# The activation sums of the seven-product scheme, all on DVE and all ahead of the first pair

## The chip, the cores and the metric

One core of a Trainium2 chip runs the whole kernel. The metric is device time in microseconds, median of several executions. The engines are named as in the profile: PE (TensorE, with PEld for its weight loads), DVE (VectorE), ACT (ScalarE), POOL (GpSimd) and SP (SyncE, whose queue issues loads).

## What is computed

The reference is one layer of a hybrid encoder on 1024 sample rows and 256 prompt rows with shared weights. The part that matters here is the MLP's first product:

```python
h2 = rms_norm(x, norm_mlp_g) * (1 + scale2) + shift2      # 1280 x 1024
x = x + gate2 * (jnp.square(jax.nn.relu(h2 @ w_mlp_up)) @ w_mlp_down)   # w_mlp_up 1024 x 4096
```

## The kernel before, in words

All large products are made from pairs: a float32 matrix is kept as a high and a low half (`h`, `l`), and each product takes three matmuls (h·h, h·l, l·h). h2, transposed, lies in `Mh[c]`, `Ml[c]` as 8 blocks k of 128 rows; chunk c = 0 and 1 are 512 sample rows each, c = 2 the 256 prompt rows.

The up product runs over 16 pairs of 128-column weight blocks. Pairs 0 and 1 are done plainly. From pair 2 on, chunks 0 and 1 together are a 2 x 2 block product done with seven block products in place of eight (`up_pair`, L1446): the activations' four blocks, B11, B21 (chunk 0, k 0 to 3 and 4 to 7), B12 and B22 (chunk 1), are combined once into T1 = B12 - B11, T2 = B22 - T1, T3 = B22 - B12 and T4 = B21 - T2, each again as high and low halves, and serve all 14 pairs. T3 is written over the first half of `Mh[1]`, `Ml[1]`. The weights' sums (`p_sum`, `p_split`) are made anew for each pair.

A set's block k (128 x 512) is made by: one sum of halves for each source block (`b_raw`, L1376, gives the float32 value back), a subtraction on DVE, a copy to the high half on ACT (`t_split`, L1389), and the low half on DVE (`t_lo`, L1390), which is issued later in the order so that DVE need not wait for ACT's copy. `t_first(k)` makes T1 and T2, `t_third(k)` T3, `t_fourth(k)` T4. Before the change, `b_raw` gives the sums of B11, B22 and B21 to POOL and that of B12 to DVE. `t_fourth` makes T2's float32 value anew from its halves, on POOL (L1413). The sums lie in a ring of five tiles of 128 x 512, `r_tile`, which also holds the up product's outputs on their way to HBM.

The order of work on each engine is written out by hand: each engine takes its instructions in program order. `t_first(0)` to `(3)` and `t_third(0)`, `(1)` stand between the evictions (`up_out`: relu, square and a DMA, all on ACT) of pairs 0 and 1 and the weight splits of pair 2 (`p_ab`: copy on ACT at L156, low half `wl` on POOL at L160). The rest stands inside pair 2, in the function `after(step)` which `up_pair` calls between its products: `t_third(2)`, `t_third(3)` after step 0, `t_fourth(0)`, `(1)` after step 1, `t_fourth(2)`, `(3)` after step 2.

In `up_pair` three small steps hold PE up if they are late. `p1` (L1457), a copy on ACT of the first product in its PSUM bank, must be made before PE adds the second product to that bank; `u2` (L1467) and `q` (L1473), DVE sums of another bank with p1, must be made before PE adds to that bank. `p1`, `u2` and `q` have one tile each in the pool `ev`. PE's work while the T sets are made is the plain products of pairs 0 and 1, then pair 2's.

Of the kernel before, what the change touches and what calls it, by code (L numbers as in the profile page):

```python
# [7 lines left out]
F32 = mybir.dt.float32  # L8
F32R = mybir.dt.float32r
AF = mybir.ActivationFunctionType  # L10
ALU = mybir.AluOpType
# [59 lines left out]
def encoder_kernel(tc, x_prompt, x_sample, c_prompt, c_sample, ada_w, ada_b, norm_mix_g, w_in,  # L71
# [3 lines left out]
    nc = tc.nc  # L75
# [10 lines left out]
    def pool(name, bufs=1, side=None, space=None):  # L86
        kw = {}
        if side:
            kw["side"] = side
        if space:  # L90
            kw["space"] = space
        if space != bass.MemoryType.DRAM:
            kw["reuse_waits"] = "tile"
        cm = tc.tile_pool(name=name, bufs=bufs, **kw)
        return cm, cm.__enter__()
# [610 lines left out]
    for part in (1, 0):  # L706
        for t in range(NT):
# [22 lines left out]
            if part == 0 and t in (2, 5):  # L730
                k = t // 3
# [256 lines left out]
    ev = {}  # L988
# [101 lines left out]
    for g in range(len(TT) + 8):  # L1090
# [5 lines left out]
        if 2 <= g < len(TT) + 2:  # L1096
            n, k = TT[g - 2]
# [13 lines left out]
    Mh = [(mcp if c == 2 else mxp).tile([128, KD, n], F32R, name=f"Mh{c}") for c, (_, n) in enumerate(CH)]  # L1111
    Ml = [(mcp if c == 2 else mxp).tile([128, KD, n], F32R, name=f"Ml{c}") for c, (_, n) in enumerate(CH)]
# [152 lines left out]
    def plain(out, ws, fi, c):  # L1265
        for k in range(KD):
            wh, wl = ws[k // 4]
            cols = slice(fi * 128, fi * 128 + 128)
            passes(out, wh[:, k % 4, cols], wl[:, k % 4, cols], Mh[c][:, k, :], Ml[c][:, k, :], k == 0, k == KD - 1)

    def up_bank():
        return bank("b", "up_ps", 8)
# [19 lines left out]
    ev_cm, ev = pool("ev", side="left")  # L1292
# [20 lines left out]
    def r_tile(name="r"):  # L1313
        return ev.tile([128, 512], F32, tag="r", name=name, bufs=5)
# [5 lines left out]
    def up_out(f, c, src, r=None):  # L1320
        r = r_tile() if r is None else r
        relu_sq(r, src)
        nc.scalar.dma_start(up_d[f][:, c * 512:c * 512 + 512], r)

    def up_out_c2(i, src):
        r = r_tile()
        relu_sq(r, src)
        for fi in range(2):
            nc.scalar.dma_start(up_d[2 * i + fi][:, 1024:T], r[:, fi * 256:fi * 256 + 256])
# [10 lines left out]
    def p_sum(i, second):  # L1340
        ra, rb = prep[i]["raw"]
        a11, a21, a12, a22 = ra[:, :, 0:128], ra[:, :, 128:256], rb[:, :, 0:128], rb[:, :, 128:256]
        s = wu.tile([128, 2, 4, 128], F32, tag="sr", name="sr", bufs=2)
        if second:
            nc.vector.tensor_tensor(s[:, 0], a11, a21, op=ALU.subtract)
            nc.vector.tensor_tensor(s[:, 1], a12, prep[i]["s12"][:, 1], op=ALU.subtract)
            prep[i]["s34"] = s
        else:
            nc.vector.tensor_tensor(s[:, 0], a21, a22, op=ALU.add)
            nc.vector.tensor_tensor(s[:, 1], s[:, 0], a11, op=ALU.subtract)  # L1350
            prep[i]["s12"] = s

    def p_split(i, second):
        prep[i]["w"]["S34" if second else "S12"] = split_w(prep[i]["s34" if second else "s12"], [128, 2, 4, 128])
# [18 lines left out]
    TT_ = {n: [Tp.tile([128, 4, 512], F32R, name=f"T{n}{x}") for x in "hl"] for n in (1, 2, 4)}  # L1373
    TT_[3] = [Mh[1][:, 0:4, :], Ml[1][:, 0:4, :]]

    def b_raw(c, k, e):  # L1376
        t = r_tile("br")
        e.tensor_tensor(t, Mh[c][:, k, :].bitcast(F32), Ml[c][:, k, :].bitcast(F32), op=ALU.add)  # L1378
        return t

    late_lo = []
# [1 line left out]
    def t_lo():  # L1383
        while late_lo:
            late_lo.pop(0)()

    def t_split(n, k, t):
        h, l = TT_[n][0][:, k, :], TT_[n][1][:, k, :]
        nc.scalar.activation(h, t, AF.Copy)  # L1389
        late_lo.append(lambda: nc.vector.tensor_tensor(l, t, h.bitcast(F32), op=ALU.subtract))  # L1390

    def t_first(k):
        b11 = b_raw(0, k, nc.gpsimd)
        b12 = b_raw(1, k, nc.vector)
        t_lo()
        b22 = b_raw(1, k + 4, nc.gpsimd)
        nc.vector.tensor_tensor(b11, b12, b11, op=ALU.subtract)
        t_split(1, k, b11)
        nc.vector.tensor_tensor(b22, b22, b11, op=ALU.subtract)
        t_lo()  # L1400
        t_split(2, k, b22)

    def t_third(k):
        b22 = b_raw(1, k + 4, nc.gpsimd)
        b12 = b_raw(1, k, nc.vector)
        t_lo()
        nc.vector.tensor_tensor(b22, b22, b12, op=ALU.subtract)
        t_split(3, k, b22)

    def t_fourth(k):  # L1410
        b21 = b_raw(0, k + 4, nc.gpsimd)
        t2 = r_tile("br")
        nc.gpsimd.tensor_tensor(t2, TT_[2][0][:, k, :].bitcast(F32), TT_[2][1][:, k, :].bitcast(F32), op=ALU.add)  # L1413
        nc.vector.tensor_tensor(b21, b21, t2, op=ALU.subtract)
        t_lo()
        t_split(4, k, b21)

    t_first(0)
    up_out(1, 0, po[1, 0])
    t_first(1)  # L1420
# [11 lines left out]
    up_out_c2(1, pm1)  # L1432
    p_sum(2, True)
    t_third(1)
    t_lo()
    up_out(2, 0, po[2, 0])
    up_out(3, 0, po[3, 0])

    def prod(out, w, at_, xh, xl, first, last, more=False):

        for k in range(4):
            a, b = k == 0 and first, k == 3 and last
            for s, (l_, r_) in enumerate(((at_(w[0], k), xh), (at_(w[0], k), xl), (at_(w[1], k), xh))):
                nc.tensor.matmul(out, lhsT=l_, rhs=r_[:, k, :], start=(a and s == 0), stop=(b and s == 2),  # L1444
                                 skip_group_check=more)

    def up_pair(i, after):
        w = prep[i]["w"]
        f0 = lambda t, k: t[:, k, 0:128]
        f1 = lambda t, k: t[:, k, 128:256]  # L1450
        s0 = lambda t, k: t[:, 0, k, :]
        s1_ = lambda t, k: t[:, 1, k, :]
        B = {(r, c): [M[c][:, 4 * r:4 * r + 4, :] for M in (Mh, Ml)] for r in range(2) for c in range(2)}
        X = up_bank()
        prod(X, w["A"], f0, *B[0, 0], True, False, True)
        p1 = ev.tile([128, 512], F32, tag="p1", name="p1", bufs=1)
        nc.scalar.activation(p1, X, AF.Copy)  # L1457
        after(0)
        pm = up_bank()
        plain(pm[:, 0:256], (w["A"], w["B"]), 0, 2)  # L1460
        prod(X, w["B"], f0, *B[1, 0], False, True, True)
        up_out(2 * i, 0, X)
        after(1)
        Y = up_bank()
        prod(Y, w["S12"], s1_, *TT_[2], True, False, True)
        u2 = ev.tile([128, 512], F32, tag="u2", name="u2", bufs=1)
        nc.vector.tensor_tensor(u2, Y, p1, op=ALU.add)  # L1467
        V = up_bank()
        prod(V, w["S12"], s0, *TT_[1], True, False, True)
        after(2)  # L1470
        prod(Y, w["S34"], s0, *TT_[3], False, False, True)
        q = ev.tile([128, 512], F32, tag="q", name="q", bufs=1)
        nc.vector.tensor_tensor(q, Y, p1, op=ALU.add)  # L1473
        c22 = r_tile()
        nc.vector.tensor_tensor(c22, V, q, op=ALU.add)
        plain(pm[:, 256:512], (w["A"], w["B"]), 1, 2)
        up_out(2 * i + 1, 1, c22, c22)
        up_out_c2(i, pm)
        after(3)
        prod(Y, w["B"], f1, *TT_[4], False, True, True)  # L1480
        c21 = r_tile()
        nc.vector.tensor_tensor(c21, Y, p1, op=ALU.add)
        up_out(2 * i + 1, 0, c21, c21)
        after(4)
        prod(V, w["S34"], s1_, Mh[1][:, 4:8, :], Ml[1][:, 4:8, :], False, True, True)
        c12 = r_tile()
        nc.vector.tensor_tensor(c12, V, u2, op=ALU.add)
        up_out(2 * i, 1, c12, c12)
        after(5)
# [27 lines left out]
    for i in range(2, NP):  # L1517
        last = i == NP - 1

        def after(step, i=i, last=last):  # L1520
            if i == 2 and step == 0:
                t_third(2)
                t_third(3)
            elif i == 2 and step < 3:
                t_fourth(2 * step - 2)
                t_fourth(2 * step - 1)
                t_lo()
            if step == 0:
                p_split(i, True)
                if last:  # L1530
                    wd_load(0)
                    wd_load(1)
                    g_load(0)
                else:
                    p_load(i + 1)
            elif step == 1:
                wd_split(0) if last else p_ab(i + 1, 0)
            elif step == 2:
                g_load(1) if last else p_sum(i + 1, False)
            elif step == 3:  # L1540
                g_split(0) if last else p_sum(i + 1, True)
            elif step == 4:
                wd_split(1) if last else p_ab(i + 1, 1)
            elif not last:
                p_split(i + 1, False)
        up_pair(i, after)
# [188 lines left out]
```

## Time and profile before

| | before |
|---|---|
| median of 3 runs | 1913.94 us (1913.16 to 1914.57) |
| the profiled execution | 1914.83 us |
| its span | 1912.9 us |
| PE, DVE, ACT, POOL busy | 97%, 56%, 36%, 37% |
| mean granted clock of PE | 0.985 |

Durations below come from the one profiled execution; its own time is 0.9 us above the median. In a row of the timeline, the first number is the start in us, the second the duration, and the bracket at the end is the idle time before it and what ended it. The granted clock is a share of full speed: 1.00 is 2.4 GHz, 0.50 is 1.2 GHz.

### The profile page before, as it was taken

How to read it: one execution, taken by the hardware profiler on the slowest of the kernel's cores; microseconds unless marked ns; L12 is line 12 of the kernel's file. 1: busy time of each engine (PE TensorE's matmuls, PEld its weight loads, DVE VectorE, ACT ScalarE, POOL GpSimd, SP SyncE). 2: the span in 40 equal slices, each digit the busy share in tenths (PEclk: the TensorE clock that was granted, in tenths of full speed). 3: DMA queues.
4: the chain of work that ended last, by engine and by line, in shares of the span. 5: the costliest groups of instructions: out<-in, count | busy, mean ns of one | idle time of the engine just before them, and what ended most of it. 6: DMA issues, size and time to landing. Idle time of an engine off the chain costs nothing.

```text
span 1912.9 us, 24543 instructions
## 1 busy us (share of the span) xinstructions
PE 1852.5 (97%) x9468; PEld 1545.5 (81%) x9468; DVE 1067.1 (56%) x1374; ACT 682.5 (36%) x1132; POOL 698.5 (37%) x517
## 2 busy tenths in 40 slices
PE   5999999999999999999999979999999999999998
PEld 2888777888997888877788868888888888888886
DVE  2799995533446777776445543333324555555557
ACT  3401111221346778773223434444444211111111
POOL 3321121421322333447312543333335543344343
PEclk7999999999999999999999989999999999999999
DMA  8313452237140212127632223222335432233224
GB/s 310 111 45 110 166 185 97 70 111 241 47 129 32 57 37 54 35 75 234 196 112 82 68 72 100 94 88 90 98 99 172 158 97 65 87 99 100 70 97 153
DMA packets 120934, 207.55 MB, mean 108 GB/s; under 512 B 10946, under 2 KB 78355, under 8 KB 119794
## 3 DMA queue, kind: packets, MB, share of 16 engines
q1 hardware_dynamic: 103106, 167.32, 27.5%
q10 hardware_dynamic: 17712, 38.67, 5.1%
q8 instruction: 74, 1.21, 0.3%
q14 instruction: 42, 0.34, 0.1%
HBM read 151.83 MB, written 54.12 MB: 108 GB/s over the span
## 4 chain that ended last, share of the span: by engine, by line
PE 54%; POOL 3%; ACT 2%; issue 2%; DVE 2%; DMA 2%; SPq 0%; ACTq 0%; POOLq 0%; DVEq 0%
PE dn_ps L1587 23%; PE up_ps L1444 13%; PE wo_ps L1198 5%; PE tp L866 2%; PE up_ps L330 1%; PE up_ps L329 1%; PE up_ps L328 1%; PE ops L881 1%; PE ops L880 1%; PE S L851 1%; PE S L850 1%; PE S L852 1%; POOL br L1378 1%; POOL wl L160 1%; DMA ga<-sig_a 1%
## 5 line engine op out<-in xcount | busy, mean ns | idle before, releaser
L160 POOL TENSOR_TENSOR wl<-wr,wh 128x1024 fp32r<-128x1024 f32 (+1 forms) x104 | 245.2, 2359 | 682.5 <-ACT wh L156 659.8
L1602 DVE TENSOR_TENSOR acc<-acc,dn_ps 128x512 f32<-128x512 f32 x260 | 178.8, 688 | 174.8 <-PE dn_ps L1587 174.8
L1587 PE MATMUL dn_ps<-wh,gl 128*128 128x512 f32 x640 | 249.1, 389 | 0.9 <-POOL gl L160 0.9
L1587 PE MATMUL dn_ps<-wl,gh 128*128 128x512 f32 x640 | 249.0, 389 | 0.0
L1587 PE MATMUL dn_ps<-wh,gh 128*128 128x512 f32 x640 | 249.0, 389 | 0.0
L156 ACT ACTIVATE wh<-wr 128x1024 fp32r<-128x1024 f32 (+1 forms) x104 | 102.9, 991 | 380.7 <-PE dn_ps L1587 289.4
L412 DVE SCALAR_TENSOR_TENSOR z<-u,dwt,z 128x1310 f32<-128x1310 f32 x120 | 220.9, 1841 | 4.4
L328 PE MATMUL fma<-Hh,wh 128*128 128x512 f32 x384 | 155.1, 404 | 0.3 <-DVE Hh L158 0.3
L329 PE MATMUL fma<-Hl,wh 128*128 128x512 f32 x384 | 150.8, 393 | 2.0 <-DVE Hl L160 2.0
L330 PE MATMUL fma<-Hh,wl 128*128 128x512 f32 x384 | 150.7, 392 | 0.0
L1587 PEld LDWEIGHTS dn_ps<-wh,gl 128*128 128x128 f32 x640 | 120.1, 188 | 26.2 <-POOL gl L160 1.4
L1587 PEld LDWEIGHTS dn_ps<-wl,gh 128*128 128x128 f32 x640 | 120.1, 188 | 25.0
L1587 PEld LDWEIGHTS dn_ps<-wh,gh 128*128 128x128 f32 x640 | 120.1, 188 | 25.0
L160 DVE TENSOR_TENSOR Pl<-tp,Ph 128x512 fp32r<-128x512 f32 x144 | 93.0, 650 | 21.6 <-ACT Ph L156 20.4
L160 POOL TENSOR_TENSOR gl<-gr,gh 128x1280 fp32r<-128x1280 f32 x32 | 94.7, 2959 | 13.7 <-DMA up_d<-r 9.7
L328 PE MATMUL up_ps<-Mh,wh 128*128 128x256 f32 (+1 forms) x320 | 97.4, 304 | 0.8 <-ACT hf L266 0.8
L1444 PE MATMUL up_ps<-Mh,wh 128*128 128x512 f32 x224 | 89.5, 399 | 8.4 <-DVE u L1467 4.3
L329 PE MATMUL up_ps<-Ml,wh 128*128 128x256 f32 (+1 forms) x320 | 97.4, 304 | 0.0
L330 PE MATMUL up_ps<-Mh,wl 128*128 128x256 f32 (+1 forms) x320 | 97.4, 304 | 0.0
L156 ACT ACTIVATE Ph<-tp 128x512 fp32r<-128x512 f32 x144 | 82.5, 574 | 37.0 <-PE tp L866 34.3
L328 PEld LDWEIGHTS fma<-Hh,wh 128*128 128x128 f32 x384 | 72.7, 189 | 23.4 <-issue 5.0
L1444 PE MATMUL up_ps<-Ml,wh 128*128 128x512 f32 x224 | 89.0, 397 | 0.0
(324 smaller groups left out, 4343.7 us busy)
## 6 DMA issues: line engine op xcount, KB each, us to landing
gr<-up_d SPq DMA_DIRECT2D x32, 640.0 KB
adr<-in_ada_w_dram SPq DMA_DIRECT2D x32, 512.0 KB
wr<-in_w_mlp_up_dram SPq DMA_DIRECT2D x32, 512.0 KB
up_d<-r ACTq DMA_DIRECT2D x64, 256.0 KB
wr<-in_w_mlp_down_dram SPq DMA_DIRECT2D x32, 512.0 KB
wr<-in_w_in_dram SPq DMA_DIRECT2D x24, 512.0 KB
ar<-in_ada_w_dram SPq DMA_DIRECT2D x8, 1024.0 KB
sig_a<-sgg ACTq DMA_DIRECT2D x8, 640.0 KB
```

Source lines behind the costliest of these rows:

```text
L156: nc.scalar.activation(h, raw, AF.Copy)
L160: e.tensor_tensor(l, raw, h.bitcast(F32), op=ALU.subtract)
L328: nc.tensor.matmul(o, lhsT=wh, rhs=xh, start=first, stop=False)
L329: nc.tensor.matmul(o, lhsT=wh, rhs=xl, start=False, stop=False)
L330: nc.tensor.matmul(o, lhsT=wl, rhs=xh, start=False, stop=last)
L412: nc.vector.scalar_tensor_tensor(out=z[j], in0=u[j][:, t:t + ZW], scalar=dwt[:, j, t:t + 1], in1=z[j], op0=ALU.mult, op1=ALU.add)
L850: nc.tensor.matmul(S[:, b:b + e], lhsT=Qh[:, qs], rhs=Kh[:, kk], start=True, stop=False)
L866: nc.tensor.transpose(tp[:, i * 128:(i + 1) * 128], st_[n]["P"][i][:, k * 128:(k + 1) * 128], ident)
L1198: nc.tensor.matmul(pp[hf], lhsT=a, rhs=wo[k][b][:, hf * 512:hf * 512 + 512], start=(k == 0 and s == 0), stop=(k == KD - 1 and s == 2))
L1444: nc.tensor.matmul(out, lhsT=l_, rhs=r_[:, k, :], start=(a and s == 0), stop=(b and s == 2), skip_group_check=more)
L1587: nc.tensor.matmul(pds[hf], lhsT=l_, rhs=r_, start=(i == 0 and s == 0), stop=(i == nf - 1 and s == 2), skip_group_check=bool(early))
L1602: nc.vector.tensor_add(acc[t][:, cs], acc[t][:, cs], pds[hf])
```

## The change

All `b_raw` sums go to DVE. In `t_first` the first three lie in the tiles p1, u2 and q of `ev`, which the pairs use only later; the fourth set is made in the same step, from T2's float32 value, which is still in the tile q. `t_third(2)` and `t_third(3)` move ahead of the first pair, `t_fourth` is gone, and `after` no longer holds any T step.

```diff
-    def b_raw(c, k, e):
-        t = r_tile("br")
-        e.tensor_tensor(t, Mh[c][:, k, :].bitcast(F32), Ml[c][:, k, :].bitcast(F32), op=ALU.add)
+    def ev_tile(tag):
+        return ev.tile([128, 512], F32, tag=tag, name=tag, bufs=1)
+
+    def b_raw(c, k, t):
+        nc.vector.tensor_tensor(t, Mh[c][:, k, :].bitcast(F32), Ml[c][:, k, :].bitcast(F32), op=ALU.add)
         return t
...
     def t_first(k):
-        b11 = b_raw(0, k, nc.gpsimd)
-        b12 = b_raw(1, k, nc.vector)
+
+        b11 = b_raw(0, k, ev_tile("p1"))
+        b12 = b_raw(1, k, ev_tile("u2"))
         t_lo()
-        b22 = b_raw(1, k + 4, nc.gpsimd)
         nc.vector.tensor_tensor(b11, b12, b11, op=ALU.subtract)
         t_split(1, k, b11)
+        b22 = b_raw(1, k + 4, ev_tile("q"))
         nc.vector.tensor_tensor(b22, b22, b11, op=ALU.subtract)
         t_lo()
         t_split(2, k, b22)
+        b21 = b_raw(0, k + 4, r_tile("br"))
+        nc.vector.tensor_tensor(b21, b21, b22, op=ALU.subtract)
+        t_lo()
+        t_split(4, k, b21)
 
     def t_third(k):
-        b22 = b_raw(1, k + 4, nc.gpsimd)
-        b12 = b_raw(1, k, nc.vector)
+        b12 = b_raw(1, k, ev_tile("u2"))
+        b22 = b_raw(1, k + 4, r_tile("br"))
         t_lo()
         nc.vector.tensor_tensor(b22, b22, b12, op=ALU.subtract)
         t_split(3, k, b22)
-
-    def t_fourth(k):
-        b21 = b_raw(0, k + 4, nc.gpsimd)
-        t2 = r_tile("br")
-        nc.gpsimd.tensor_tensor(t2, TT_[2][0][:, k, :].bitcast(F32), TT_[2][1][:, k, :].bitcast(F32), op=ALU.add)
-        nc.vector.tensor_tensor(b21, b21, t2, op=ALU.subtract)
-        t_lo()
-        t_split(4, k, b21)
...
     up_out_c2(1, pm1)
     p_sum(2, True)
     t_third(1)
+    t_third(2)
+    t_third(3)
     t_lo()
     up_out(2, 0, po[2, 0])
     up_out(3, 0, po[3, 0])
...
         def after(step, i=i, last=last):
-            if i == 2 and step == 0:
-                t_third(2)
-                t_third(3)
-            elif i == 2 and step < 3:
-                t_fourth(2 * step - 2)
-                t_fourth(2 * step - 1)
-                t_lo()
             if step == 0:
```

## Rows read from the trace of the kernel before

**Rows 1.** The page: busy us of each engine (share of the span) and instructions
```profile
PE 1852.5 (97%) x9468; PEld 1545.5 (81%) x9468; DVE 1067.1 (56%) x1374; ACT 682.5 (36%) x1132; POOL 698.5 (37%) x517
```

**Rows 2.** Windows: stretch, length, busy us of the engines, granted clock, DMA share, GB/s
```profile
1056.00:1099.60 43.60, 43.60 (x216) 37.02 (x215) 26.74 (x31) 20.58 (x32) 26.41 (x17) 1.00 0.20 67
1099.60:1144.80 45.20, 32.77 (x133) 26.76 (x132) 22.98 (x29) 16.31 (x26) 19.81 (x14) 0.81 0.22 70
1144.80:1169.70 24.90, 24.90 (x134) 21.56 (x133) 7.63 (x9) 10.57 (x16) 9.55 (x4) 1.00 0.30 96
1169.70:1194.50 24.80, 24.80 (x134) 21.48 (x132) 7.69 (x9) 10.73 (x16) 9.55 (x4) 1.00 0.30 96
```

**Rows 3.** Timeline of PE through pair 2, to the start of pair 3
```profile
1099.60 0.39 PE L1444 MATMUL up_ps<-Mh,wh 128*128 128x512 f32 x1
...
1105.07 0.28 PE L330 MATMUL up_ps<-Mh,wl 128*128 128x256 f32 x1
1109.40 0.80 PE L1444 MATMUL up_ps<-Mh,wh 128*128 128x512 f32 x1 [4.05 <-ACT p L1457]
...
1124.87 0.47 PE L1444 MATMUL up_ps<-Mh,wh 128*128 128x512 f32 x1 [4.30 <-DVE u L1467]
...
1136.39 0.77 PE L1444 MATMUL up_ps<-T4h,wh 128*128 128x512 f32 x1 [4.07 <-DVE q L1473]
...
1144.82 0.39 PE L1444 MATMUL up_ps<-Mh,wh 128*128 128x512 f32 x1
```

**Rows 4.** Windows after the third idle stretch of PE
```profile
1136.00:1142.00 6.00, 5.61 (x13) 4.47 (x14) 2.25 (x5) 2.49 (x4) 0.00 (x0) 0.50 0.50 150
```

**Rows 5.** Timeline of ACT ahead of the first p1
```profile
1104.91 0.63 ACT L1389 ACTIVATE Mh<-br 128x512 fp32r<-128x512 f32 x1 [1.23 <-DVE br L1407]
1105.45 0.58 ACT L1317 ACTIVATE r<-up_ps 128x512 f32<-128x512 f32 x1
...
1108.75 0.60 ACT L1457 ACTIVATE p<-up_ps 128x512 f32<-128x512 f32 x1 [0.40 <-ACT r L1318]
```

**Rows 6.** Timeline of DVE in the chain of the T sets
```profile
1060.69 0.69 DVE L1378 TENSOR_TENSOR br<-Mh,Ml 128x512 f32<-128x512 f32 x1
1069.18 1.75 DVE L1397 TENSOR_TENSOR br<-br 128x512 f32<-128x512 f32 x1 [7.81 <-POOL br L1378]
...
1090.33 0.69 DVE L1390 TENSOR_TENSOR T1l<-br,T1h 128x512 fp32r<-128x512 f32 x1
1090.93 0.68 DVE L1349 TENSOR_TENSOR sr<-wr 128x512 f32<-128x512 f32 x1
1091.65 0.69 DVE L1350 TENSOR_TENSOR sr<-sr,wr 128x512 f32<-128x512 f32 x1
1092.26 2.89 DVE L1378 TENSOR_TENSOR br<-Mh,Ml 128x512 f32<-128x512 f32 x1
1095.07 0.68 DVE L1390 TENSOR_TENSOR T2l<-br,T2h 128x512 fp32r<-128x512 f32 x1
...
1111.25 0.68 DVE L1407 TENSOR_TENSOR br<-br 128x512 f32<-128x512 f32 x1
```

**Rows 7.** Instructions on the tiles br: count, ns min/median/max, first and last start
```profile
L1378 POOL TENSOR_TENSOR br<-Mh,Ml x16: 1272/1288/1740, 1067.9 to 1129.2; 128x512 f32<-128x512 f32 x16
...
L1413 POOL TENSOR_TENSOR br<-T2h,T2l x4: 1277/1469/1740, 1117.2 to 1130.5; 128x512 f32<-128x512 f32 x4
```

**Rows 8.** Timeline of POOL: the first, the fourth and the fifth of five splits
```profile
1062.90 2.40 POOL L160 TENSOR_TENSOR wl<-wr,wh 128x1024 fp32r<-128x1024 f32 x1 [2.74 <-ACT wh L156]
...
1092.11 2.49 POOL L160 TENSOR_TENSOR wl<-wr,wh 128x1024 fp32r<-128x1024 f32 x1 [3.65 <-ACT wh L156]
1096.44 2.39 POOL L160 TENSOR_TENSOR wl<-sr,wh 128x1024 fp32r<-128x1024 f32 x1 [1.84 <-ACT wh L156]
```

**Rows 9.** Instructions of line 1602 after 1500 us, beside POOL's splits in the down product
```profile
L1602 DVE TENSOR_TENSOR acc<-acc,dn_ps x248: 686/687/689, 1500.5 to 1836.4; 128x512 f32<-128x512 f32 x124
```

More of the change, by code (lines that the diff above doesn't have):

```diff
@@ L1455, in up_pair @@
         prod(X, w["A"], f0, *B[0, 0], True, False, True)
-        p1 = ev.tile([128, 512], F32, tag="p1", name="p1", bufs=1)
+        p1 = ev_tile("p1")
         nc.scalar.activation(p1, X, AF.Copy)
@@ L1465, in up_pair @@
         prod(Y, w["S12"], s1_, *TT_[2], True, False, True)
-        u2 = ev.tile([128, 512], F32, tag="u2", name="u2", bufs=1)
+        u2 = ev_tile("u2")
         nc.vector.tensor_tensor(u2, Y, p1, op=ALU.add)
@@ L1471, in up_pair @@
         prod(Y, w["S34"], s0, *TT_[3], False, False, True)
-        q = ev.tile([128, 512], F32, tag="q", name="q", bufs=1)
+        q = ev_tile("q")
         nc.vector.tensor_tensor(q, Y, p1, op=ALU.add)
```

## The prediction

> **What bounds the kernel now.** I read the page's busy times first: PE is busy for 97% of the span [rows 1]. So a change to the helper engines is worth only what it takes out of PE's idle time, or out of the time PE runs at the lower clock, and the question is where PE is not full. The stretches around the change answer it [rows 2]: from 1056 to 1099.6 us PE is busy throughout at a granted clock of 1.00; in the pair i = 2, from 1099.6 to 1144.8, it is busy 32.77 of 45.2 us at a mean granted clock of 0.81; in the next pair it is full again at 1.00 for 24.9 us. PE's own rows place both ends: the first product of pair 2 starts at 1099.60, the same product of pair 3 at 1144.82 [rows 3], 45.2 us apart, where a full pair takes 24.8 (24.9 and 24.8 in the next two windows [rows 2]). Pair 2 therefore carries **20.4 us** of loss, and this is all the change can win.
>
> The loss has two parts. PE stands idle three times: 4.05 us before 1109.40, released by ACT's copy p (p1); 4.30 us before 1124.87, released by DVE's u (u2); 4.07 us before 1136.39, released by DVE's q [rows 3]. Sum 12.4. The remaining 8.0 us is the clock: after an idle stretch it is granted at 0.50, which is 1.2 GHz in place of 2.4, as in 1136 to 1142 [rows 4]. Three spells, 8.0 us, 2.7 us each on average.
>
> Why these three are late: p1, u2 and q are themselves short; they are stuck in order behind transform work. p1 stands on ACT behind the copy Mh of t_third(1), then two up_out; that copy waited 1.23 us for its DVE subtraction [rows 5]. u2 and q stand on DVE behind t_fourth's steps, which wait for POOL. The chain on DVE starts at 1060.69, then its next instruction waits 7.81 us for a POOL sum, and runs 1.75 us [rows 6] where 0.68 is usual. POOL does 16 sums at L1378 and 4 at L1413 [rows 7].
>
> **The change, part by part.**
>
> *Taken off POOL.* Twenty sums with medians of 1.29 and 1.47 us, some 27 us of POOL [rows 7]. POOL was never PE's direct releaser here, so this by itself is worth nothing; what counts is that DVE no longer waits for a POOL result. Those waits go to zero by construction: no DVE instruction of the chain has a POOL operand any more.
>
> *Added to DVE.* 16 sums: b11, b22 and b21 four times each, and b22 of t_third four times. The four sums that rebuilt the second set from its halves disappear, since b22 still lies in SBUF. DVE instructions follow each other 0.60 us apart, and 0.72 where one reads the result of the one before it (1090.33 to 1090.93 to 1091.65 [rows 6]).
>
> *Blocked by the weight splits.* POOL keeps its splits wl. A DVE sum of two SBUF tiles that met one took 2.89 us and the next instruction started 2.81 us after it (1092.26, 1095.07 [rows 6]), while the split ran from 1092.11 for 2.49 us [rows 8]; that is 2.2 us over the usual 0.60. Five splits lie in the chain, from 1062.90 to 1096.44 [rows 8] (those of pair 1's two halves, of pair 2's two halves, and of S12). DVE will now be working without a break, so I charge all five: 11.0 us.
>
> *Moved.* t_fourth goes into t_first, and t_third(2) and (3) go from after(0) to before the first pair. In program order every T copy then stands on ACT ahead of up_out(2,0), up_out(3,0) and p1, and every T step on DVE ahead of u2 and q. This removes what u2 and q waited for and lengthens what p1 waits for: the PE wait moves into one place. No DMA is added; p_load(3) on the SP queue still waits for the second p_sum(2), which stays where it is in the DVE order, before t_third(1). Nothing goes to the POOL queue. The new waits on p1, u2 and q as scratch tiles are on ACT copies and DVE steps that come earlier in the same chain; they cost nothing as long as each copy is done two DVE instructions later (1.2 us against the copy's 0.63 [rows 5]).
>
> *The sum for p1.* The last subtraction of t_third(3) is the 59th DVE instruction from 1060.69: 9 in each t_first, four delayed low halves of T4, 4 of the p_sums, and 12 sums and subtractions with 3 low halves of t_third. 58 steps of 0.60 are 34.8; ten steps read the instruction just ahead, 0.12 more each, 1.2; five splits 11.0. Together 47.0, so it starts at 1107.7 and ends at 1108.4. From there ACT repeats the sequence seen before: copy Mh at 1104.91, two up_out, p1 at 1108.75 for 0.60 [rows 5], 4.4 us. p1 ends at 1112.8 and PE goes on at 1112.9. It ran out at 1105.35 (last matmul at 1105.07, 0.28 long [rows 3]): **idle 7.6 us**. After that nothing is queued ahead of u2 and q but two p_sum steps, T3 is complete by about 1109, and S12's split is done long before; the S34 split follows p1 on ACT and has about 8 us (three products of 12 matmuls, 2.7 us each) before it is read. So the second and third idle stretches go. One idle stretch instead of three means one spell at 0.50: 2.7 us.
>
> New loss 7.6 + 2.7 = 10.3, against 20.4: **10.1 us won**. What is late next is p1 still, now behind DVE's own chain.
>
> Does PE run dry earlier, where it is full now? The B half of pair 2 is split after t_first(3). By the same count that is DVE's 38th instruction: 1060.69 + 37 times 0.60 + 9 times 0.12 + three splits of 2.2, 1090.6; the copy and the split (2.49) end by about 1095, and PE reads that half after 1103. Slack 8 us, cost nothing. The T copies that overwrite Mh[1] come after 1097, PE's last plain product on that chunk ended long before.
>
> *Bounds.* If only three splits block (the first two come while ACT is still busy with copies and DVE may wait anyway), idle shrinks by 4.4 and 14.5 us are won. If each step takes its full 0.68 instead of 0.60, 58 steps are 4.6 longer, which absorbs the 1.2: 6.7 won. The clock spell may be 1.7 to 3.7 (one of the three spells against the mean): plus or minus 1. I keep the middle, since DVE in the uninterrupted run of rows 6 goes at 0.60.
>
> One rule of the Trainium skill speaks against the direction: "Perfetto Trace Analysis", Optimizing Scalar/DVE Operations, says that where DVE is saturated it may help to hand work to GpSimd, and adds that the two share an SBUF read port, so it might not. The trace bears out the second half: a sum on POOL kept DVE's subtraction at 1.75 us, 1.07 over its 0.68, more than the 0.60 that doing the sum on DVE costs. The first half is a rival below.
>
> **The base.** The profiled execution took 1914.83 us for a span of 1912.9; the median of the runs is 1913.94, 0.9 below. 1914.83 - 10.1 = 1904.7 for a like profile; on the median, **1903.8**.
>
> **Rivals.**
>
> *All of it goes* (1893.5, chance 0.05). If splits on POOL did not hold up DVE, the last subtraction would end 11.0 earlier, near 1097.4, p1 would wait only for its product, and pair 2 would take 24.8 us: 20.4 won. For it: 248 DVE additions at L1602 run beside POOL's splits at 686 to 689 ns, none lengthened [rows 9]. Against: these read PSUM; the chain's instructions read two SBUF tiles, as the one of 2.89 us did.
>
> *The hand-offs between DVE and ACT take the place of the POOL waits* (slower, 1915.2 at full size, chance 0.04; part of it within 0.2%, 0.07). Each of the 16 T copies lies on ACT between a DVE subtraction and a DVE low half. If each low half waited out the whole turn (copy 0.63 and the two hand-overs, 0.7), the chain would be 11.4 longer, idle 19.0, loss 21.7, 1.3 over the present. It turns to a loss from 0.63 us per copy. For it: ACT also holds six up_out and four weight copies in this stretch. Against: two DVE instructions stand between each subtraction and its low half, and the up_outs' banks are ready long before ACT gets to them.
>
> *DVE is saturated, and the sums are only added work* (slower, 1921.7, chance 0.03). If taking the sums off POOL released nothing, DVE would do 12 steps of the fourth set and 12 more sums ahead of where the last t_third subtraction now is, 1111.25 [rows 6]: ends 1111.9 + 24 times 0.60 = 1126.3, p1 4.4 later, idle 25.5, with the spell 28.2, 7.8 over the present 20.4. This is what the skill's rule on a saturated DVE would mean here. Against: DVE's idle waits for POOL sums, 7.81 us in one place alone [rows 6], are of the same size as the additions.
>
> **How the numbers follow.** The forecast holds 0.81, with its own range of 1900 to 1908. What a measurement of this kernel can tell from no change is about 0.2%, 3.8 us. Faster: 0.81 + 0.05 = 0.86; within 0.2%: 0.07; slower: 0.04 + 0.03 = 0.07. The range for 8 in 10: from 1900 (three splits and some clock) to 1909 (each step at 0.68, a spell of 3.7, and a part of the hand-offs).
>
> **What would show it.** In the changed kernel DVE should be busy without a wait for POOL from 1061 to about 1108, with up to five instructions of 2 to 3 us, each beside a wl split. PE should have one idle stretch in pair 2, released by p (p1), of 6 to 10 us from 1105.4, followed by one stretch at 0.50, and none released by u or q. Pair 3's first product should start near 1134.7. I am wrong if p1 is on time, if DVE shows waits for ACT copies summing to several us, if PE stops before 1099, or if an idle stretch ahead of the T2, T3 or T4 products remains.

## The result and the profile after

| | before | after |
|---|---|---|
| median | 1914.26 us (4 runs) | 1904.57 us (4 runs) |
| all runs | 1913.16 to 1915.13 | 1904.15 to 1904.88 |
| the profiled execution | 1914.83 | 1904.15 |
| its span | 1912.9 | 1902.1 |
| DVE, POOL instructions | 1374, 517 | 1390, 497 |

The change made the kernel faster: ratio 0.995, 95% interval 0.9932 to 0.9967. That is 9.7 us on the medians and 10.8 between the two profiled spans; the text below goes by the spans, since the rows come from them.

The page's busy times after, to be read against [rows 1]: DVE has 16 instructions more, POOL 20 fewer, PE's busy time is 7.0 us shorter for the same 9468 matmuls. Of that, 6.2 us (32.77 to 26.58) lie in pair 2: time that it no longer spends at the lower clock.

```profile
PE 1845.5 (97%) x9468; PEld 1541.8 (81%) x9468; DVE 1076.8 (57%) x1390; ACT 682.3 (36%) x1132; POOL 674.3 (35%) x497
```

The windows after (stretch, length, busy PE, PEld, DVE, ACT, POOL, granted clock, DMA share, GB/s). The first answers the first of [rows 2], the second is pair 2 exactly:

```profile
1056.00:1099.60 43.60, 43.60 (x216) 37.07 (x215) 42.18 (x54) 24.63 (x39) 15.40 (x8) 1.00 0.20 67
...
1099.45:1133.90 34.45, 26.58 (x133) 22.68 (x132) 16.68 (x23) 11.92 (x20) 5.24 (x3) 0.90 0.28 92
```

PE is still full up to pair 2, while DVE in that stretch has gone from 26.74 to 42.18 us of 43.60. Pair 2 takes 34.45 us where it took 45.2; a full pair takes 24.85, so its loss has fallen from 20.4 to 9.6 us. The difference, 10.8, is the whole difference of the spans: on balance nothing was won or lost elsewhere.

PE's timeline in pair 2 after (start, duration, the bracket is idle time and what ended it), beside [rows 3]. Where three idle stretches stood there is one, before the product that waits for p1. The T2 product at 1117.42, the T3 product (on Mh, at 1122.87) and the T4 product at 1128.46 start without a bracket:

```profile
1104.92 0.28 PE L330 MATMUL up_ps<-Mh,wl 128*128 128x256 f32 x1
1113.07 0.79 PE L1445 MATMUL up_ps<-Mh,wh 128*128 128x512 f32 x1 [7.87 <-ACT p L1458]
1113.66 0.63 PE L1445 MATMUL up_ps<-Ml,wh 128*128 128x512 f32 x1
...
1117.42 0.40 PE L1445 MATMUL up_ps<-T2h,wh 128*128 128x512 f32 x1
...
1122.87 0.39 PE L1445 MATMUL up_ps<-Mh,wh 128*128 128x512 f32 x1
...
1128.46 0.40 PE L1445 MATMUL up_ps<-T4h,wh 128*128 128x512 f32 x1
...
1133.93 0.39 PE L1445 MATMUL up_ps<-Mh,wh 128*128 128x512 f32 x1
```

DVE's chain after: its first step, the five steps that met a split, and the last subtraction. [rows 6] show it before, with 7.81 us of waiting for POOL behind the first step. Now DVE's only wait in the chain is 0.69 us for the last ACT copy, behind the last subtraction:

```profile
1060.55 0.69 DVE L1380 TENSOR_TENSOR p<-Mh,Ml 128x512 f32<-128x512 f32 x1
...
1063.20 2.78 DVE L1402 TENSOR_TENSOR q<-q,p 128x512 f32<-128x512 f32 x1
1065.91 2.87 DVE L1392 TENSOR_TENSOR T1l<-p,T1h 128x512 fp32r<-128x512 f32 x1
1068.71 0.68 DVE L1380 TENSOR_TENSOR br<-Mh,Ml 128x512 f32<-128x512 f32 x1
...
1078.70 2.88 DVE L1399 TENSOR_TENSOR p<-u,p 128x512 f32<-128x512 f32 x1
1081.51 0.68 DVE L1380 TENSOR_TENSOR q<-Mh,Ml 128x512 f32<-128x512 f32 x1
...
1092.96 2.89 DVE L1380 TENSOR_TENSOR u<-Mh,Ml 128x512 f32<-128x512 f32 x1
1095.77 0.68 DVE L1380 TENSOR_TENSOR br<-Mh,Ml 128x512 f32<-128x512 f32 x1
...
1097.58 2.88 DVE L1345 TENSOR_TENSOR sr<-wr 128x512 f32<-128x512 f32 x1
1100.39 0.68 DVE L1346 TENSOR_TENSOR sr<-wr,sr 128x512 f32<-128x512 f32 x1
...
1107.86 0.68 DVE L1414 TENSOR_TENSOR br<-br,u 128x512 f32<-128x512 f32 x1
1109.24 0.69 DVE L1392 TENSOR_TENSOR Ml<-br,Mh 128x512 fp32r<-128x512 f32 x1 [0.69 <-ACT Mh L1391]
```

From step to step the five cost 2.71, 2.80, 2.81, 2.81 and 2.81 us in place of 0.60. ACT's end of the chain after (compare [rows 5]): the last copy waits 1.90 us for the subtraction above, then come the two evictions, then p1. From the copy's start to p1's end it is 4.44 us, as before:

```profile
1108.58 0.63 ACT L1391 ACTIVATE Mh<-br 128x512 fp32r<-128x512 f32 x1 [1.90 <-DVE br L1414]
1109.11 0.58 ACT L1317 ACTIVATE r<-up_ps 128x512 f32<-128x512 f32 x1
...
1112.42 0.60 ACT L1458 ACTIVATE p<-up_ps 128x512 f32<-128x512 f32 x1 [0.40 <-ACT r L1318]
```

### The profile page after: what moved, and what is told of

Read it like the earlier page. It is cut to its first block, busy times and chain, and to the rows that moved or that the text cites. A ratio compares the mean times of both kernels' runs of the same rounds, so it can differ in the third digit from the quotient of the medians.

```text
span 1902.1 us, 24518 instructions
## 1 busy us (share of the span) xinstructions
PE 1845.5 (97%) x9468; PEld 1541.8 (81%) x9468; DVE 1076.8 (57%) x1390; ACT 682.3 (36%) x1132; POOL 674.3 (35%) x497
## 4 chain that ended last, share of the span: by engine, by line
PE 54%; DVE 4%; DMA 2%; ACT 2%; POOL 2%; issue 2%; SPq 0%; ACTq 0%; POOLq 0%; DVEq 0%
PE dn_ps L1581 23%; PE up_ps L1445 14%; PE wo_ps L1198 4%; PE tp L866 2%; PE up_ps L330 2%; PE up_ps L329 2%; PE up_ps L328 2%; PE ops L881 1%; PE ops L880 1%; PE S L851 1%; PE S L850 1%; PE S L852 1%; DMA ga<-sig_a 1%; POOL m L1151 1%; ACT P L858 0%
## 5 line engine op out<-in xcount | busy, mean ns | idle before, releaser
L1468 DVE TENSOR_TENSOR u<-up_ps,p 128x512 f32<-128x512 f32 x14 | 9.7, 691 | 146.0 <-ACT wh L156 146.0
```

## The experiments

The theory to be tested has two halves. The gain comes from the engine: DVE no longer waits for POOL's sums nor is held up by them. And the order takes part of it back: with every T set ahead of the pair, p1 waits behind DVE's whole chain, which is long because five weight splits hold it up. The rivals: the order is what wins; or the splits' hold-up is absorbed and the number of steps sets the chain.

### Only the engine changed: old_order_dve

The kernel before, with its order and its fourth set from the halves, and `nc.vector` for all twenty POOL sums:

```diff
-        b11 = b_raw(0, k, nc.gpsimd)
+        b11 = b_raw(0, k, nc.vector)
...
-        nc.gpsimd.tensor_tensor(t2, TT_[2][0][:, k, :].bitcast(F32), TT_[2][1][:, k, :].bitcast(F32), op=ALU.add)
+        nc.vector.tensor_tensor(t2, TT_[2][0][:, k, :].bitcast(F32), TT_[2][1][:, k, :].bitcast(F32), op=ALU.add)
```

> The order of the kernel before (t_third(2), (3) and t_fourth inside pair 2, the second set's sum taken from its halves again), only the engine changed: all 20 POOL sums on DVE. Theory (the engine is what counts, and the moving ahead is what makes p1 late): p1 on time, no idle stretch before it, u2 within 1 us of its time, and one idle stretch of about 4 us before the T4 product, behind q, because DVE has two T4 blocks and two weight sums between u2 and q; with a spell at the lower clock about 1901 to 1902, faster than the changed kernel. Rival (the order carries the gain, the engine little): 1908 or more, with waits before p1 and u2 as before.

Measured: median 1899.53 us (1897.37 to 1901.0), ratio to before 0.9927 (0.9912 to 0.9942). That is 5 us faster than the full change. Its PE timeline has no wait for p1 and these two idle stretches:

```profile
1112.33 0.47 PE L1444 MATMUL up_ps<-Mh,wh 128*128 128x512 f32 x1 [0.24 <-DVE u L1467]
1121.55 0.47 PE L1444 MATMUL up_ps<-T4h,wh 128*128 128x512 f32 x1 [3.35 <-DVE q L1473]
```

The place of the remaining wait is the one expected, its length 3.35 us for 4. No spell at the lower clock follows in this execution, which is the fastest of the four:

```profile
1120.00:1125.00 5.00, 3.45 (x15) 2.92 (x16) 3.70 (x7) 2.26 (x4) 0.00 (x0) 1.00 0.14 30
```

That spell was part of the 1901 to 1902 that were expected; whether its absence also explains the median, 1.5 to 2.5 us below that, is not shown, since the other three runs have no trace. So the engine alone is worth 14 us, and the rival that the order carries the gain falls.

### Only the order changed: sums_pool

The changed kernel, with the sums of b11, b22 and b21, and b22 of t_third, on POOL; the fourth set still comes from the second in SBUF:

```diff
-    def b_raw(c, k, t):
-        nc.vector.tensor_tensor(t, Mh[c][:, k, :].bitcast(F32), Ml[c][:, k, :].bitcast(F32), op=ALU.add)
+    def b_raw(c, k, t, e=nc.gpsimd):
+        e.tensor_tensor(t, Mh[c][:, k, :].bitcast(F32), Ml[c][:, k, :].bitcast(F32), op=ALU.add)
...
-        b12 = b_raw(1, k, ev_tile("u2"))
+        b12 = b_raw(1, k, ev_tile("u2"), nc.vector)
```

> The order of the changed kernel (all sets ahead of pair 2, the fourth from the second), only the engine undone: the 16 sums that were added to DVE run on POOL. Theory (each POOL sum holds up a two-input DVE step by about 1.1 us, and DVE waits for POOL's results): the chain ends about 11 us later than in the changed kernel, one idle stretch before p1 of about 19 us: 1914 to 1918, no faster than the kernel before. Rival (the moving ahead and the saved fourth-set sums carry the gain): 1904 to 1908.

Measured: 1914.46 us, ratio 1.0007 (0.9998 to 1.0017): no faster than before. PE has one idle stretch, the predicted 19 us, and behind it a product of 12 matmuls that takes 5.3 us (1123.19 to 1128.47) where 2.7 is usual:

```profile
1123.19 0.80 PE L1445 MATMUL up_ps<-Mh,wh 128*128 128x512 f32 x1 [18.97 <-ACT p L1458]
...
1128.47 0.63 PE L1445 MATMUL up_ps<-T2h,wh 128*128 128x512 f32 x1
...
1131.62 0.39 PE L1445 MATMUL up_ps<-T1h,wh 128*128 128x512 f32 x1
```

The first rows of DVE's chain in this run show the wait for POOL and the hold-up beside POOL's sums:

```profile
1059.55 0.68 DVE L1380 TENSOR_TENSOR u<-Mh,Ml 128x512 f32<-128x512 f32 x1
1068.04 1.75 DVE L1399 TENSOR_TENSOR p<-u,p 128x512 f32<-128x512 f32 x1 [7.80 <-POOL p L1380]
```

The order of the change gains nothing without the engine. It folds three idle stretches of 12.4 us in all into one of 19.0, and three spells of 8.0 us in all into one of about 3.0 (5.3 and 3.15 us for two products of 2.7): pair 2 loses about 22 us where it lost 20.4.

### The cost of the five splits: splits_zero

The changed kernel; the low halves of the first five splits are zeros written by POOL, so that part of the weights' product is left out:

```diff
-        hi_lo(h, l, raw, "a", "g")
+        ring["n"] += 1
+        if ring["n"] <= 5:
+            nc.scalar.activation(h, raw, AF.Copy)
+            nc.gpsimd.memset(l.bitcast(F32), 0.0)
+        else:
+            hi_lo(h, l, raw, "a", "g")
```

> The changed kernel, but the low halves of the first five weight splits (both halves of pairs 1 and 2, and S12 of pair 2) are set to zero by POOL, which reads nothing, instead of being the difference of two SBUF tiles; that part of the computation is left out. Theory (the five splits hold DVE up by 2.2 us each, 11 us in the chain): DVE's chain runs at 0.60 to 0.72 us a step, its last t_third subtraction ends near 1098, p1 follows its product, no idle stretch in pair 2: about 1895. Rival (the splits' hold-up is absorbed elsewhere, the count of steps sets the chain): idle before p1 stays 6 to 8 us, 1903 to 1905.

Measured: 1893.46 us, ratio 0.9897 (0.9882 to 0.9912). PE is full in pair 2 and the next:

```profile
1099.40:1124.30 24.90, 24.90 (x134) 21.58 (x133) 8.53 (x11) 10.73 (x17) 4.79 (x2) 1.00 0.23 74
```

DVE's timeline, the first step of the chain with what stands ahead of it, and the last subtraction:

```profile
1059.54 3.25 DVE L158 CAST Mh<-hf 128x256 fp32r<-128x256 f32 x1 [0.40 <-ACT hf L266]
...
1063.16 0.68 DVE L1385 TENSOR_TENSOR p<-Mh,Ml 128x512 f32<-128x512 f32 x1
...
1099.58 0.68 DVE L1419 TENSOR_TENSOR br<-br,u 128x512 f32<-128x512 f32 x1
```

The chain starts 2.6 us later than in the changed kernel, because three of POOL's zero fills now come early and DVE's last cast of h2, 3.25 us long, ran beside them; for that reason the last subtraction ends at 1100.3 and not near 1098. From there it takes 36.4 us to the last subtraction, where it took 47.3: the difference, 10.9 us, is what the five splits cost the chain after the change, and no step in it is longer than 0.69 us. It ends 8.3 us earlier, more than the 7.9 us that PE had waited. Without the splits' hold-up p1 is thus on time even in this order; the rival that it is absorbed falls.

### The order repaired: third123_late

The changed kernel, with t_third(1) to (3) behind p1 and behind the S34 split's copy:

```diff
     t_third(0)
     up_out_c2(1, pm1)
     p_sum(2, True)
-    t_third(1)
-    t_third(2)
-    t_third(3)
     t_lo()
     up_out(2, 0, po[2, 0])
     up_out(3, 0, po[3, 0])
...
             if step == 0:
                 p_split(i, True)
+                if i == 2:
+                    t_third(1)
+                    t_third(2)
+                    t_third(3)
+                    t_lo()
```

> The changed kernel, but t_third(1), (2) and (3) stand in after(0), behind p1 and behind the S34 split's copy, instead of ahead of up_out(2,0). Theory (p1 is late only because it stands on ACT behind the copies of t_third, which wait for DVE's long chain): p1 follows its product, PE has no idle stretch at 1105, and no spell at the lower clock; DVE's chain is as long as before, so the last T3 low half still comes near 1110, ahead of the product that reads it (about 1113.3). The 9.6 us that pair 2 still loses in the changed kernel go: about 1895. Rival (the DVE chain is too long for pair 2 wherever it stands): the idle stretch moves to the T3 product and is 3 to 8 us: 1898 to 1904.

Measured: 1894.46 us (1893.77 to 1895.0), ratio 0.9901 (0.9885 to 0.9918): 10.1 us faster than the change, at the same arithmetic. p1 runs at 1103.32, ahead of the end of the product that PE has in between, and the product that waits for p1 starts without a bracket. The one idle stretch that is left in pair 2 is the last row of PE here:

```profile
1103.32 0.60 ACT L1455 ACTIVATE p<-up_ps 128x512 f32<-128x512 f32 x1 [0.40 <-ACT r L1318]
```

```profile
1104.63 0.40 PE L1442 MATMUL up_ps<-Mh,wh 128*128 128x512 f32 x1
...
1113.16 0.47 PE L1442 MATMUL up_ps<-Mh,wh 128*128 128x512 f32 x1 [0.18 <-DVE u L1465]
```

```profile
1111.72 0.69 DVE L1392 TENSOR_TENSOR Ml<-br,Mh 128x512 fp32r<-128x512 f32 x1 [0.70 <-ACT Mh L1391]
1112.33 0.68 DVE L1465 TENSOR_TENSOR u<-up_ps,p 128x512 f32<-128x512 f32 x1
```

The last T3 step ends at 1112.4, u2 follows it at once, and PE waits 0.18 us. DVE's chain still takes some 52 us; it only no longer stands ahead of p1. The rival (too long wherever it stands) falls, by a narrow margin: T3 and u2 are now just in time.

### Half of the repair: third23_back

Only t_third(2) and (3) go back behind p1:

```diff
     t_third(1)
-    t_third(2)
-    t_third(3)
...
+            if i == 2 and step == 0:
+                t_third(2)
+                t_third(3)
+                t_lo()
             if step == 0:
```

> The changed kernel, with t_third(2) and (3) put back into after(0), behind p1; t_third(1) stays ahead of the two evictions. Theory (p1's lateness is the time by which DVE's chain up to the last t_third ahead of it is late): the copy for t_third(1) starts at 1103.5 and not 1108.6, so p1 comes 5.1 us earlier, the idle stretch before it is 2.8 us instead of 7.9, and the spell at the lower clock shrinks or is gone: 1897.5 to 1899.5. Rival (the gain needs t_third(1) moved too, or what is put back delays the T3 product): 1900 or more, with an idle stretch before the T3 product.

Measured: 1896.95 us (1896.69 to 1897.78), ratio 0.9914 (0.9899 to 0.9929). This is 0.5 us below the range that was expected. The idle stretch is the predicted one, and the clock stays at 1.00 behind it:

```profile
1107.26 0.50 PE L1443 MATMUL up_ps<-Mh,wh 128*128 128x512 f32 x1 [2.89 <-ACT p L1456]
```

```profile
1106.00:1111.00 5.00, 3.74 (x16) 3.10 (x17) 3.28 (x5) 3.24 (x6) 0.25 (x1) 1.00 0.14 55
```

7.87 - 2.89 = 5.0 us less idle time and 1.7 of the spell are 6.7. The spans differ by 7.4 and the medians by 7.6; 0.8 us of the rest is that the whole stretch ran earlier (the copy of t_third(1) at 1102.71 against 1103.51). So p1's time follows the last t_third ahead of it, as the theory has it.

### The clock's part alone: filler

The changed kernel, with 24 matmuls into an unread PSUM bank ahead of the product that waits for p1:

```diff
+        if i == 2:
+            fill = up_bank()
+            plain(fill, (w["A"], w["B"]), 0, 0)
         prod(X, w["B"], f0, *B[1, 0], False, True, True)
```

> The changed kernel, with 24 more matmuls of 512 columns on PE in pair 2 ahead of the product that waits for p1, into a PSUM bank that nobody reads. Theory (the idle stretch costs its length and, behind it, a spell at the granted clock 0.50, 8 matmuls at twice their spacing): the fillers take 5.5 us of the 7.9, the product still starts at about 1113 because p1 sets it, the idle rest of about 2.4 us brings no spell, and pair 2 is 1.6 to 1.8 us shorter: about 1902.8, by the profile's own span 1.7 less than the changed kernel. Rival (the spell is a cost of that place, not of the idle stretch, or the fillers delay p1): no gain, or a loss of up to 5.5.

Measured: 1903.22 us, ratio 0.9947 (0.993 to 0.9963); the span is 1901.4 against 1902.1. The fillers fit and did not delay p1, but the spell did not go:

```profile
1112.33 0.50 PE L1445 MATMUL up_ps<-Mh,wh 128*128 128x512 f32 x1 [2.42 <-ACT p L1458]
```

```profile
1113.00:1116.00 3.00, 3.00 (x9) 2.36 (x8) 0.00 (x0) 0.22 (x1) 2.37 (x1) 0.51 0.00 0
```

The product starts 0.74 us earlier than in the changed kernel because the whole stretch does (the copy ahead of p1 at 1107.83 against 1108.58), which is the 0.7 of the span. The gain expected from the clock was not there: this is a miss, and the run doesn't tell what the spell costs, since it removed none of it. It came out as its rival has it, that the spell belongs to the place and not to the idle stretch; but in third23_back the same product, behind 2.89 us of idle time, runs without a spell, so the place alone does not bring one either.

## Why the prediction was right

Forecast 1903.8 us, measured 1904.57, inside 1900 to 1909; 10.1 us won were forecast and 9.7 measured. Step by step:

- **Where the loss lies.** Right. All of the 10.8 us between the spans is in pair 2.
- **The engine.** Right, and the experiments apportion it: the engine alone gains 14 us (old_order_dve), the order alone nothing (sums_pool), together 9.7. Part of what the engine gains is given back by the order (the four sums that the change saves are counted with it). What leaves with POOL's sums is both DVE's waits for them (7.81 us in one place [rows 6]) and its hold-up beside them (1.75 us for 0.68); no run separates the two.
- **DVE's chain.** Forecast 47.0 us from its first step to the start of the last subtraction, measured 47.3 (1060.55 to 1107.86). Twelve steps, not ten, read the instruction just ahead, which adds 0.24. Of the 47.3 the splits were put at 11.0 and measured at 10.9: 13.94 for the five steps less 3.0 for five usual ones.
- **p1.** Forecast to end at 1112.8 and PE to go on at 1112.9; measured 1113.02 and 1113.07. Idle 7.6 forecast, 7.87 measured.
- **u2 and q.** Right: neither is a releaser of PE after. The S34 split had the room it was given: POOL ended it at 1116.4, and the product that reads it starts at 1122.87.
- **The clock.** The term that was mis-sized: 2.7 us for the spell, measured 1.7 (9.6 of loss less 7.87 idle). The mean of the three earlier spells stood in for a single one; the low bound, 1.7, would have been the value. That a spell came at all was not assured: the prediction counts one for each idle stretch, and the stretches of 2.89 us (third23_back) and 3.35 us (old_order_dve) had none.
- **The base.** The median moved 1.1 us less than the spans did. By the spans the loss terms were forecast 0.7 too high, by the medians the gain 0.4 too high; both are near the spread of the runs. The forecast took the median to lie 0.9 us below the profiled execution, as it did before; after the change it lies 0.4 above (1904.57, 1904.15). So 1.3 us here and 0.3 of idle time were forecast too low and 1.0 of the spell too high: that the forecast stands only 0.8 us from the measured median is in part these misses offsetting each other.

Of the rivals, "all of it goes" had its condition named rightly: it needed the splits not to hold DVE up, and splits_zero, where they don't, takes 1893.46 against the 1893.5 worked out (closer than its own runs, 1893.08 to 1894.32, allow one to claim). The hand-offs between DVE and ACT did not show: one wait for a copy, 0.69 us. The rival of a saturated DVE had one half right, DVE is saturated in this stretch (42.18 of 43.60 us), and the other wrong: it waits for POOL no longer, and sums_pool shows that giving the sums back to POOL costs 9.9 us. The Trainium skill ("Perfetto Trace Analysis", Optimizing Scalar/DVE Operations) says that handing work to GpSimd may make sense where DVE is saturated, and adds that it might not help, since the two share an SBUF read port. The runs bear out only the reservation: beside a sum on POOL, DVE's subtraction took 1.75 us for 0.68 (sums_pool).

What the prediction did not ask was whether the forecast idle stretch could be moved behind other work. The row that it rested on, p1 behind two evictions and a copy that waits for DVE, already pointed there: third123_late wins the other 10 us by moving three calls.

## What to carry to other kernels

When a helper's work moves from one engine to another, cost the chain on the engine that receives it, with each instruction of the old engine that still runs beside it, and then look in program order for the one short instruction behind it on which PE waits. Moving work ahead "to have it done" moves it ahead of everything else on its in-order engine too; place it just before its own reader, behind the short steps that PE needs sooner. Try the engine and the order separately: here, on medians, one was worth 14 us and the other, on top of it, cost 5.

## What was not expected of the hardware

The length of PE's idle stretch alone did not tell whether a spell at the lower clock (0.50, 1.2 GHz) follows. In the profiled executions a stretch of 2.42 us was followed by one (filler: granted 1.00 up to 1113, 0.7 us after the product's start, and 0.51 in the three us from there), while stretches of 2.89 us (third23_back) and 3.35 us (old_order_dve) were followed by none. Nor did the length of the stretch order the cost of the spell: behind 7.87 us it cost 1.7 us, behind the three of about 4 us before the change 2.7 on average, and behind the 18.97 us of sums_pool about 3.0. What else decides it is left open; no run was made for it. The other runs of old_order_dve took 1899.31 to 1901.0, 1.9 to 3.6 us above the profiled one. A spell in them would fit that, but they have no trace, and their mean granted clock, 0.989 to 0.990 against 0.989 in the profiled run, does not show one.

What POOL does decides which DVE instruction it holds up. In splits_zero a DVE cast with one input took 3.25 us (1059.54, shown above) beside POOL's first zero fills, which read nothing. The same cast took 0.29 us with POOL idle, and 0.57 beside one of POOL's short subtractions; in both held-up cases it ended 0.15 us after POOL. The two-input sums of the chain ran at 0.69 us beside the fills that came later:

```profile
1057.80 0.57 DVE L158 CAST Mh<-hf 128x256 fp32r<-128x256 f32 x1 [0.40 <-ACT hf L266]
...
1058.85 0.29 DVE L158 CAST Mh<-hf 128x256 fp32r<-128x256 f32 x1
...
1069.56 0.69 DVE L1385 TENSOR_TENSOR u<-Mh,Ml 128x512 f32<-128x512 f32 x1
```

```profile
1057.48 0.74 POOL L160 TENSOR_TENSOR Ml<-hf,Mh 128x256 fp32r<-128x256 f32 x1 [1.00 <-DVE Mh L158]
...
1059.90 2.74 POOL L1308 MEMSET wl<- 128x1024 f32 x3
1069.37 0.95 POOL L1308 MEMSET wl<- 128x1024 f32 x1 [6.72 <-PE up_ps L330]
1072.09 0.96 POOL L1308 MEMSET wl<- 128x1024 f32 x1 [1.76 <-PE up_ps L330]
```

In the changed kernel, beside a POOL split, which reads two tiles, DVE's two-input instructions took 2.78 to 2.89 us. The Trainium skill, "SBUF — State Buffer", SBUF: two separate sides, says that a DVE instruction with two SBUF inputs excludes only a GpSimd instruction that reads SBUF, while one in a two-port mode excludes any. The rows agree with the first part, and the casts with the second, if they run in such a mode, which no row shows.
